# Gate products of a two-layer encoder: results kept in PSUM banks, the sigmoid table loaded earlier, products issued in a fixed order

## The chip, the core and the metric

The kernel runs on one core of one Trainium2 chip. A core has five engines with their own queues, each working strictly in its own order: TensorE (PE, matmuls; its weight loads are listed apart as PEld), VectorE (DVE), ScalarE (ACT), GpSimd (POOL) and SyncE (SP), which here only issues DMA transfers. Matmuls write into PSUM banks; everything else lies in SBUF. The metric is the device time of one execution in microseconds (us).

## The reference, and what is computed

The model is a trunk of two layers over 512 tokens of width 1024. Each layer adds the output of a token mixer (neighbourhood attention in layer 0, latent attention in layer 1) to the residual, and then adds a gated embedding. A final RMSNorm follows. The part that this case is about:

```python
h = x + y
gate = jax.nn.sigmoid(rmsnorm(h, ple_norm[i]) @ ple_w_gate[i])
x = h + gate * (p[i] @ ple_w_proj[i])
...
return rmsnorm(x, final_norm)
```

All is float32. The kernel splits every operand of a matmul into a rounded part ("hi") and the remainder ("lo") and computes hi x hi + lo x hi + hi x lo.

## The kernel before, in words

Layer 0 and the attention of layer 1 fill the first 600 us or so and are not touched. In layer 1 the gate's matmul `rmsnorm(h) @ ple_w_gate` (512 x 1024 by 1024 x 1024) is done with seven products of quarter size in place of eight (`gate_seven`, L571). The 512 rows are two halves of two row tiles; `i` = 0, 1 is the row tile within a half. Each product `p` has a left operand `X[p]` (a quarter of the turned `h`, or a sum or difference of quarters) and a right operand `W[p]` (a quarter of the weight, or a sum of quarters that was added up in DRAM earlier). They run in the order 1, 7, 6, 5, 4, 3, 2.

What feeds them:

- `out_proj` (L416) is the projection before it: its matmuls go out at L107, its sums into `res` at L428, and after each piece `turn_h` (L1011) multiplies by the gain (L1016), transposes on TensorE (L139, tag "T" of PSUM) and hands the bank to `keep_half` (L541), which copies or adds the quarters (L553 to L562). `operand` (L532) makes the hi part on ACT (L538) and the lo part on DVE (L539); `mixed` (L564) does so for products 6, 5, 4 and 3, with one more subtraction (L568) for 3.
- `prep` (L578) fetches the two pieces of a weight: a DMA from SP's queue into one of three buffers `wraw`, the hi part on ACT (L589), the lo part on POOL (L590). A buffer is free again when POOL has read it. The loop at L612 calls `prep` three products ahead.
- The matmuls (L634): twelve for each product and row tile, 512 columns wide. For products 1 and 2 of row tile 1 the columns are cut into two halves of 256.

What becomes of them: product 1 is copied out by ACT (`s1`, L639); product 7 is added to it by DVE (`s17`, L644); product 6 is copied out by ACT (`s6`, L647), and product 5 then goes on accumulating in the bank of 6 (tag "S"), and product 3 in the same bank again; product 2 goes on in the bank of product 1 (tag "mm", and "O" for the last half). `quarter` (L602) adds or subtracts the needed sums (L604, DVE), and `finish` (L593) does the rest of one quarter: the sigmoid (L594, ACT, scaled by the row's inverse norm `rh`), the load of the projection's piece `pe` (L596, SP), the product (L597, DVE) and the sum into the residual `r` (L599, DVE). The result of L604, L594 and L597 is a tile `g` in SBUF. Last, `done` (L1049) sums the squares of the finished row (L1060 on ACT, L1056 on DVE for the very last half), collects the mean (L1061), multiplies by the final gain (L1064 on POOL for the half of a row that is ready first, L1071 on DVE for the other), takes the power -0.5 on POOL (L1070), scales on ACT (L1072) and sends the row out (L1073, L1074).

The order of work on each engine isn't the order of the program's text. The Tile layer orders the instructions with a planning run of its own; `issue_after(x)` forbids it to place an instruction ahead of `x`. PSUM tiles are taken from rings by tag: "mm" has two banks, "S" two, "T" three, "O" one; a tile waits until the last reader of the tile that had its bank is through.

In the kernel before, the planning run mixes products on TensorE: ten of the twelve matmuls of product 6, row tile 0, go before product 7, parts of product 4 between those of product 6, and product 4 of row tile 0 before product 5.

Of the kernel before, what the change touches and what calls it, by code (L numbers as in the profile page):

```python
# [13 lines left out]
F32 = mybir.dt.float32  # L14
F32R = mybir.dt.float32r
AF = mybir.ActivationFunctionType
ALU = mybir.AluOpType
AX = mybir.AxisListType
PSUM = bass.MemoryType.PSUM
P = 128  # L20
S = 512
# [19 lines left out]
class Trunk:  # L41
# [374 lines left out]
    def out_proj(self, wap, oT, res, after, last_mm):  # L416
        nc = self.nc
        for n in range(2):
            ws = [self.load_w(wap[n, c], 1024, extra=n == 1 or c == 3) for c in range(4)]
            for u, t in enumerate((0, 2, 1, 3) if n and self.wxn > 5 else range(NT)):  # L420
                ps = self.psum(("mm", "mm", "S", "S", "T", "O", "mm", "mm")[n * NT + u])
                L = lambda s, k: oT[s][k // 4][:, k % 4, t * P:(t + 1) * P]
                W = lambda s, k: ws[k // 2][s][:, (k % 2) * S:(k % 2 + 1) * S]
                m = self.by_chunk(L, W)
                with self.tc.issue_after(last_mm):
                    self.mms(ps, m)
                r = res[t][:, n * S:(n + 1) * S]
                nc.vector.tensor_tensor(out=r, in0=ps, in1=r, op=ALU.add)  # L428
                after(t, n)
# [141 lines left out]
    def gate_seven(self, pool, layer, rh, res, after):  # L571

        nc = self.nc
        pieces = 0
        turns = 3 + self.wxn // 2
        W, A, Bk, s1, s17, s6 = {}, {}, {}, {}, {}, {}

        def prep(p):  # L578
            nonlocal pieces
            W[p] = []  # L580
            src = self.quarter[layer][p] if p < 4 else self.sums[layer][p]
            for c in range(2):
                own = pieces % turns < 3
                pieces += 1
                raw = self.wp.tile([P, 1024], F32, name="wraw", tag="wraw", bufs=3)
                q, n = (self.wp, 3) if own else (pool, self.wxn)
                hi, lo = (q.tile([P, 1024], F32R, name=t, tag=t if own else "w4", bufs=n) for t in ("whi", "wlo"))
                nc.sync.dma_start(raw, src[c * P:(c + 1) * P])
                nc.scalar.activation(hi, raw, AF.Copy)  # L589
                nc.gpsimd.tensor_tensor(out=lo, in0=raw, in1=hi.bitcast(F32), op=ALU.subtract)  # L590
                W[p].append((hi, lo))

        def finish(t, n, x, src, o=0, wd=S):  # L593
            nc.scalar.activation(x, src, AF.Sigmoid, scale=rh[t])  # L594
            pe = pool.tile([P, S], F32, name="pe", tag="pe", bufs=4)[:, :wd]
            nc.sync.dma_start(pe, self.pe[layer][t][:, n * S + o:n * S + o + wd])  # L596
            nc.vector.tensor_tensor(out=x, in0=pe, in1=x, op=ALU.mult)  # L597
            r = res[t][:, n * S + o:n * S + o + wd]
            nc.vector.tensor_tensor(out=r, in0=r, in1=x, op=ALU.add)  # L599
            after(t, n, o, wd)  # L600

        def quarter(t, n, ps, other, op):  # L602
            x = pool.tile([P, S], F32, name="g", tag="hg", bufs=3)
            nc.vector.tensor_tensor(out=x, in0=ps, in1=other, op=op)  # L604
            finish(t, n, x, x)

        order = (1, 7, 6, 5, 4, 3, 2)
        whole, parts = ((0, S),), ((0, 256), (256, 256))
        for p in order[:3]:
            prep(p)  # L610
        self.mixed(6)
        for k, p in enumerate(order):  # L612
            if k + 3 < len(order):
                prep(order[k + 3])
            if 0 < k < 4:
                self.mixed(order[k + 2])
            x = self.X[p]
            for i in range(2):
                cuts = parts if layer == 1 and i == 1 and p < 3 else whole
                if p == 1:  # L620
                    A[i] = [self.psum("O" if o else "mm") for o, wd in cuts]
                elif p in (7, 6, 4):
                    ps = self.psum({7: "T", 6: "S", 4: "T"}[p])
                    if p == 6:
                        Bk[i] = ps
                else:
                    ps = Bk[i]
                for h, (o, wd) in enumerate(cuts):
                    if p < 3:
                        ps = A[i][h]  # L630
                    m = [(x[:, 2 * s + i, k * P:(k + 1) * P], W[p][k // 2][r][:, k % 2 * S + o:k % 2 * S + o + wd])
                         for c in range(2) for s, r in ((0, 0), (1, 0), (0, 1)) for k in (2 * c, 2 * c + 1)]
                    for j, (l, r) in enumerate(m):
                        nc.tensor.matmul(ps[:, :wd], l, r, start=j == 0 and p in (1, 7, 6, 4),  # L634
                                         stop=j == 11 and p not in (1, 6, 5), skip_group_check=True)
                    if p == 1:
                        if o == 0:
                            s1[i] = self.temp("s1")
                        nc.scalar.activation(s1[i][:, o:o + wd], ps[:, :wd], AF.Copy)  # L639
                    elif p == 2:  # L640
                        finish(i, 0, pool.tile([P, S], F32, name="g", tag="hg", bufs=3)[:, :wd], ps[:, :wd], o, wd)
                    elif p == 7:
                        s17[i] = self.temp("s17")
                        nc.vector.tensor_tensor(out=s17[i], in0=ps, in1=s1[i], op=ALU.add)  # L644
                    elif p == 6:
                        s6[i] = self.temp("s6")
                        nc.scalar.activation(s6[i], ps, AF.Copy)  # L647
                    elif p == 5:
                        quarter(2 + i, 1, ps, s17[i], ALU.subtract)
                        nc.gpsimd.tensor_tensor(out=s6[i], in0=s17[i], in1=s6[i], op=ALU.subtract)  # L650
                    elif p == 4:
                        quarter(2 + i, 0, ps, s6[i], ALU.add)
                    else:
                        quarter(i, 1, ps, s1[i], ALU.subtract)

    def mla_c(self, pool, xT, cT, sets):
        nc, a = self.nc, self.a
# [533 lines left out]
```

## Time and profile before

| what | time |
|---|---|
| median of 3 runs | 670.32 us (670.09 to 671.56) |
| the profiled execution | 669.8 us |
| its span on the core | 668.0 us |
| PE / DVE / ACT / POOL busy | 652.5 / 383.1 / 422.3 / 421.4 us |
| mean granted clock of TensorE | 0.991 |

The profile is of one execution. Its page lists busy time by engine, the span in slices, the chain of waits that ended last, and groups of instructions. The timeline has one row for each run of equal instructions: start and length in us, engine, line of the code, operation, result and inputs, shapes, count, and in brackets how long the engine was idle before it and what ended that. A row of the view of stretches has the stretch, its length, and busy time and count of PE, PEld, DVE, ACT and POOL, then the granted TensorE clock, the DMA share and GB/s.

### The profile page before, as it was taken

To read this page: it belongs to the slowest core of one execution; us is meant where nothing else is said; L and a number is where in the kernel's file an instruction comes from. 1 tells how busy PE (TensorE), PEld (TensorE's weight loads), DVE (VectorE), ACT (ScalarE), POOL (GpSimd) and SP (SyncE) were. 2 spreads that over 40 slices of the span, in tenths; PEclk is the share of its full clock that TensorE was granted. 3 is DMA by queue.
4 is the path that set the end of the run, shared out by engine and by line. 5 is a ranking of instruction groups with operands and counts; after the bars stand their busy time and mean duration, and the time that the engine had idled before them with its cause. 6 is when DMAs were issued, how large, how long until landed. Compare 5 with 4: busy or idle time off the path is not lost.

```text
span 668.0 us, 10021 instructions
## 1 busy us (share of the span) xinstructions
PE 652.5 (98%) x3443; PEld 555.5 (83%) x3443; DVE 383.1 (57%) x817; ACT 422.3 (63%) x837; POOL 421.4 (63%) x340
## 2 busy tenths in 40 slices
PE   9999999999999999999999999999999999999991
PEld 6888888988988888888899888888888888888881
DVE  6180375737645515544615514888888875067867
ACT  7661686848767742543434636888989887347745
POOL 0395466876575765943155616886969785858773
PEclk9999999999999999999999999999999999999996
DMA  9949323966142146533343244110301232764323
GB/s 330 335 150 350 135 92 99 201 155 156 58 142 76 64 148 245 190 104 137 107 115 108 90 120 141 54 46 25 90 7 69 60 111 95 275 235 163 131 79 142
DMA packets 37682, 90.63 MB, mean 136 GB/s; under 512 B 4416, under 2 KB 13376, under 8 KB 37568
## 3 DMA queue, kind: packets, MB, share of 16 engines
q1 hardware_dynamic: 33040, 85.02, 37.3%
q0 software_dynamic: 4160, 4.19, 4.0%
q10 hardware_dynamic: 432, 0.79, 0.3%
q8 instruction: 27, 0.44, 0.3%
q14 instruction: 23, 0.19, 0.1%
HBM read 78.45 MB, written 16.78 MB: 143 GB/s over the span
## 4 chain that ended last, share of the span: by engine, by line
PE 91%; DVE 2%; POOL 2%; issue 2%; DMA 1%; ACT 1%; POOLq 0%; DVEq 0%
PE ps_mm L107 42%; PE ps_S L107 13%; PE ps_mm L721 6%; PE ps_T L139 6%; PE ps_O L832 4%; PE ps_T L107 3%; PE ps_O L107 3%; PE ps_T L238 2%; PE ps_O L402 2%; PE ps_mm L184 2%; PE ps_T L390 2%; PE ps_S L354 1%; PE ps_S L353 1%; DVE r L599 1%; PE ps_O L238 1%
## 5 line engine op out<-in xcount | busy, mean ns | idle before, releaser
L84 POOL TENSOR_TENSOR wwlo<-wraw,wwhi 128x1024 fp32r<-128x1024 f32 (+5 forms) x93 | 178.6, 1934 | 106.3 <-ACT wwhi L83 91.4
L83 ACT ACTIVATE wwhi<-wraw 128x1024 fp32r<-128x1024 f32 (+5 forms) x94 | 79.1, 863 | 74.4 <-PE ps_mm L107 18.3
L817 POOL TENSOR_TENSOR ex<-ex,rc 128x512 f32<-128x512 f32 x64 | 65.9, 1038 | 24.8 <-DVE rc L816 18.1
L815 ACT ACTIVATE ex<-ps_S,mx 128x512 f32<-128x512 f32 x64 | 44.0, 688 | 11.9 <-DVE mx L813 10.8
L813 DVE TENSOR_REDUCE mx<-ps_S 128x1 f32<-128x512 f32 x64 | 43.7, 682 | 6.8 <-PE ps_S L107 6.2
L96 DVE TENSOR_TENSOR pt_lo<-ps_T,pt_hi 128x512 fp32r<-128x512 f32 x64 | 43.2, 681 | 7.6 <-ACT pt_hi L94 7.3
L376 POOL TENSOR_TENSOR ex<-ex,rc 128x128 f32<-128x128 f32 (+1 forms) x64 | 34.8, 582 | 18.2 <-DVE rc L372 18.2
L107 PE MATMUL ps_mm<-xh,wwhi 128*128 128x512 f32 x152 | 40.9, 399 | 0.0
L94 ACT ACTIVATE pt_hi<-ps_T 128x512 fp32r<-128x512 f32 x64 | 37.7, 595 | 4.1 <-PE ps_T L139 3.8
L590 POOL TENSOR_TENSOR wlo<-wraw,whi 128x1024 fp32r<-128x1024 f32 x14 | 36.4, 2619 | 3.2 <-ACT whi L589 3.2
L139 PE MATMUL ps_T<-ident,ex 128*128 128x128 f32 x256 | 38.4, 272 | 0.0
L107 PE MATMUL ps_mm<-xl,wwhi 128*128 128x512 f32 x152 | 38.3, 391 | 0.0
L107 PE MATMUL ps_mm<-xh,wwlo 128*128 128x512 f32 x152 | 38.0, 390 | 0.0
L139 PEld LDWEIGHTS ps_T<-ident,ex 128*128 128x128 f32 x256 | 31.5, 140 | 7.7 <-POOL ex L817 0.4
L107 PE MATMUL ps_mm<-wwhi,hnT 128*128 128x512 f32 x128 | 35.0, 392 | 0.0
L205 DVE TENSOR_TENSOR u<-ps_O,u 64x512 f32<-64x512 f32 x32 | 22.0, 686 | 20.1 <-ACT u L204 19.6
L107 PEld LDWEIGHTS ps_mm<-xl,wwhi 128*128 128x128 f32 x152 | 28.4, 188 | 5.9
L107 PEld LDWEIGHTS ps_mm<-xh,wwlo 128*128 128x128 f32 x152 | 28.3, 188 | 5.8
L370 ACT ACTIVATE ex<-ex,mx 128x128 f32<-128x128 f32 (+1 forms) x64 | 30.2, 474 | 1.8 <-DVE mx L360 0.8
L107 PEld LDWEIGHTS ps_mm<-xh,wwhi 128*128 128x128 f32 x152 | 27.4, 188 | 4.8
L107 PE MATMUL ps_S<-ke,qe 96*128 96x512 f32 x96 | 28.9, 407 | 0.0
L107 PE MATMUL ps_S<-ko,qo 128*128 128x512 f32 x96 | 28.9, 409 | 0.0
(423 smaller groups left out, 1783.4 us busy)
## 6 DMA issues: line engine op xcount, KB each, us to landing
wraw<-na_qk SPq DMA_DIRECT2D x16, 512.0 KB, 3.2
pe<-pe SPq DMA_DIRECT2D x31, 256.0 KB, 2.8
wraw<-gate SPq DMA_DIRECT2D x14, 512.0 KB, 3.2
wraw<-na_v SPq DMA_DIRECT2D x8, 512.0 KB, 3.3
wraw<-na_o SPq DMA_DIRECT2D x8, 512.0 KB, 3.3
wraw<-mla_z SPq DMA_DIRECT2D x8, 512.0 KB, 3.5
wraw<-mla_o SPq DMA_DIRECT2D x8, 512.0 KB, 3.4
wraw<-sum SPq DMA_DIRECT2D x8, 512.0 KB, 3.2
```

Source lines behind the costliest of these rows:

```text
L83: nc.scalar.activation(hi[:, c], raw[:, c], AF.Copy)
L84: f = lambda e, c=c: e.tensor_tensor(out=lo[:, c], in0=raw[:, c], in1=hi[:, c].bitcast(F32), op=ALU.subtract)
L94: self.last_copy = nc.scalar.activation(hi, src, AF.Copy, scale=scale)
L96: nc.vector.tensor_tensor(out=lo, in0=src, in1=hi.bitcast(F32), op=ALU.subtract)
L107: last = self.last_mm = nc.tensor.matmul(out, l, r, start=i == 0, stop=i == n - 1)
L139: self.last_mm = self.nc.tensor.transpose(t[:, i * P:(i + 1) * P], b, self.ident)
L376: self.last_norm = nc.gpsimd.tensor_tensor(out=e, in0=e, in1=rc[:, qt:qt + 1].to_broadcast([P, e.shape[1]]), op=ALU.mult)
L590: nc.gpsimd.tensor_tensor(out=lo, in0=raw, in1=hi.bitcast(F32), op=ALU.subtract)
L721: self.last_mm = nc.tensor.matmul(PS[key], *terms[i], start=i == 0, stop=i == len(terms) - 1)
L813: nc.vector.reduce_max(mx, sp, axis=AX.X, negate=True)
L815: nc.scalar.activation(ex, sp, AF.Exp, bias=mx, accum_out=sm)
L817: nc.gpsimd.tensor_tensor(out=ex, in0=ex, in1=rc.to_broadcast([P, S]), op=ALU.mult)
```

## The change

It has these parts:

- `finish` works in place: sigmoid, product with `pe` and the sum's input stay in the PSUM bank that `quarter` (or product 2's matmuls) left them in. For products 4 and 3 the sum of the quarter is written back into the product's own bank; for product 5 it is written into a new bank of tag "T", since product 3 goes on accumulating in product 5's bank. The SBUF tile `g` is gone.
- A one-column sigmoid `warm` stands in front of the loop, so the sigmoid table is loaded there and not at the first quarter's sigmoid.
- Each matmul of the products carries `issue_after` of the one before it, and the first that of `out_proj`'s last: TensorE issues the products in the loop's order.
- The `prep` of a product is called one turn of the loop later for the last three (product 4's, 3's and 2's): before, `order[k + 3]` at turn k; now product 5 at turn 0, and `order[k + 2]` from turn 2 on.

```diff
-                    self.mms(ps, m)
+                    self.last_out = self.mms(ps, m)
...
-        def finish(t, n, x, src, o=0, wd=S):
-            nc.scalar.activation(x, src, AF.Sigmoid, scale=rh[t])
+        def finish(t, n, x, o=0, wd=S):
+            nc.scalar.activation(x, x, AF.Sigmoid, scale=rh[t])
...
-        def quarter(t, n, ps, other, op):
-            x = pool.tile([P, S], F32, name="g", tag="hg", bufs=3)
+        def quarter(t, n, x, ps, other, op):
             nc.vector.tensor_tensor(out=x, in0=ps, in1=other, op=op)
-            finish(t, n, x, x)
-
+            finish(t, n, x)
+
+        mm = self.last_out
...
         self.mixed(6)
+        warm = self.small.tile([P, 1], F32, name="warm", tag="warm", bufs=1)
+        nc.scalar.activation(warm, rh[3], AF.Sigmoid)
         for k, p in enumerate(order):
-            if k + 3 < len(order):
-                prep(order[k + 3])
+            if k == 0:
+                prep(order[3])
+            if k > 1 and k + 2 < len(order):
+                prep(order[k + 2])
...
-                        nc.tensor.matmul(ps[:, :wd], l, r, start=j == 0 and p in (1, 7, 6, 4),
-                                         stop=j == 11 and p not in (1, 6, 5), skip_group_check=True)
+                        with self.tc.issue_after(mm.ins):
+                            mm = nc.tensor.matmul(ps[:, :wd], l, r, start=j == 0 and p in (1, 7, 6, 4),
+                                                  stop=j == 11 and p not in (1, 6, 5), skip_group_check=True)
...
-                        finish(i, 0, pool.tile([P, S], F32, name="g", tag="hg", bufs=3)[:, :wd], ps[:, :wd], o, wd)
+                        finish(i, 0, ps[:, :wd], o, wd)
...
-                        quarter(2 + i, 1, ps, s17[i], ALU.subtract)
+                        quarter(2 + i, 1, self.psum("T"), ps, s17[i], ALU.subtract)
...
-                        quarter(2 + i, 0, ps, s6[i], ALU.add)
+                        quarter(2 + i, 0, ps, ps, s6[i], ALU.add)
...
-                        quarter(i, 1, ps, s1[i], ALU.subtract)
+                        quarter(i, 1, ps, ps, s1[i], ALU.subtract)
```

In the built programs the engines' orders are the same up to the products. From there: TensorE has the last four transposes (L139) right behind product 1 and the products in the loop's order. On ACT the table load and `warm` stand behind the hi part of product 4's second weight piece, which itself now comes behind the hi part of `X[6]`, row tile 1. On DVE the two subtractions from the last transposes (L560, L561) and the second L568 stand ahead of the lo parts of `X[4]` and `X[3]`, row tile 0; further on, L597 and L599 of one quarter follow each other directly, where before several quarters' steps were interleaved. POOL's order is the same. On SP the load of the last `pe` piece (256 columns) stands behind two output transfers.

More of the change, by code (lines that the diff above doesn't have):

```diff
@@ L589, in prep @@
                 nc.scalar.activation(hi, raw, AF.Copy)
-                nc.gpsimd.tensor_tensor(out=lo, in0=raw, in1=hi.bitcast(F32), op=ALU.subtract)
+                nc.gpsimd.tensor_tensor(out=lo, in0=raw, in1=hi.bitcast(F32),
+                                                                             op=ALU.subtract)
                 W[p].append((hi, lo))
-        def finish(t, n, x, src, o=0, wd=S):
-            nc.scalar.activation(x, src, AF.Sigmoid, scale=rh[t])
+        def finish(t, n, x, o=0, wd=S):
+            nc.scalar.activation(x, x, AF.Sigmoid, scale=rh[t])
             pe = pool.tile([P, S], F32, name="pe", tag="pe", bufs=4)[:, :wd]
```

## The prediction, made before the changed kernel was run

> **What bounds the kernel now.** I read the page first, then the stretches of the last 50 us, because the order of instructions before about 613 us is the same in both kernels on every engine; only the quarter products and what follows them change.
>
> ```profile
> 630.00:640.00 10.00, 10.00 (x46) 8.28 (x45) 3.04 (x5) 6.57 (x9) 8.57 (x5) 1.00 0.24 86
> 650.00:660.00 10.00, 3.61 (x28) 3.29 (x26) 9.77 (x19) 7.16 (x16) 5.48 (x5) 0.83 0.40 145
> ```
>
> After the stretch and its length come PE, weight load, VectorE (DVE), ScalarE (ACT) and GpSimd (POOL). TensorE is full at 630 to 640, at a granted clock of 1.00, and has 3.61 us of work left after 650 (its last row, below, ends at 653.6); the span ends at 668.0. So some 14 us are a tail, in which DVE is full (9.77 of 10), while at 630 to 640 it was busy only 3.04. DVE starts late, and then works slowly. The timeline says why:
>
> ```profile
> 636.99 0.69 DVE L604 TENSOR_TENSOR g<-ps_S,s 128x512 f32<-128x512 f32 x1 [4.64 <-PE ps_S L634]
> 637.62 1.06 ACT L589 ACTIVATE whi<-wraw 128x1024 fp32r<-128x1024 f32 x1 [3.40 <-POOL s L650]
> 638.70 1.28 ACT L594 ACT_TABLE_LOAD   x1
> 640.00 0.72 ACT L594 ACTIVATE g<-g,rs 128x512 f32<-128x512 f32 x1
> 640.75 1.02 DVE L597 TENSOR_TENSOR g<-pe,g 128x512 f32<-128x512 f32 x1 [3.08 <-ACT g L594]
> 641.81 2.77 DVE L599 TENSOR_TENSOR r<-r,g 128x512 f32<-128x512 f32 x1
> 641.18 2.85 POOL L590 TENSOR_TENSOR wlo<-wraw,whi 128x1024 fp32r<-128x1024 f32 x1
> 646.03 1.22 DVE L597 TENSOR_TENSOR g<-pe,g 128x512 f32<-128x512 f32 x1 [0.19 <-ACT g L594]
> 650.85 1.12 DVE L599 TENSOR_TENSOR r<-r,g 128x512 f32<-128x512 f32 x1
> 656.38 1.63 DVE L599 TENSOR_TENSOR r<-r,g 128x512 f32<-128x512 f32 x1
> 659.54 1.42 DVE L599 TENSOR_TENSOR r<-r,g 128x256 f32<-128x256 f32 x1
> 661.35 0.41 DVE L599 TENSOR_TENSOR r<-r,g 128x256 f32<-128x256 f32 x1
> 661.92 0.49 DVE L1056 CUSTOM_DVE_ANT_0 sq<-r,mn 128x256 f32<-128x256 f32 x1
> 662.49 0.99 POOL L1070 TENSOR_TENSOR rs<-mn,half 128x1 f32<-128x1 f32 x1 [0.33 <-DVE mn L1056]
> 663.52 0.75 DVE L1071 SCALAR_TENSOR_TENSOR r<-r,rs,gn 128x512 f32<-128x512 f32 x1 [0.44 <-POOL rs L1070]
> ```
>
> The first quarter's sum is there at 637.68, yet its sigmoid starts at 640.00, behind a weight piece and a table load on ACT. Then L599 takes 2.77 us for what L604 does in 0.69. It ends at 644.58, and the POOL row that it overlaps at 644.03: 0.55 later. Wherever a DVE operation with both inputs in SBUF meets a POOL operation, it ends some 0.55 after POOL; L604, with one input in PSUM, never stretches.
>
> **The change, part by part.** Below, P5.0 means product 5 for row tile i = 0.
>
> *Results in PSUM.* Sum, sigmoid and product of each quarter now stand in a bank, so L597 and L599 each have one SBUF input. What the six stretched rows lose goes: 0.34 + 2.09 + 0.54 + 0.44 + 0.95 + 1.01 = 5.4 us (each against 0.68, the last against 0.41). All six lie in the stretches where DVE is full. Not all of it reaches the end, because the matmuls and the handovers come next; the walk below finds how much.
>
> *Price of an operand in PSUM.* The groups by form give, behind the bar, busy us and the mean ns of one:
>
> ```profile
> L594 ACT ACTIVATE g<-ps_mm,rs 128x512 f32<-128x512 f32 x1 | 0.7, 667 | 0.0
> L594 ACT ACTIVATE g<-ps_mm,rs 128x256 f32<-128x256 f32 x1 | 0.5, 462 | 0.0
> ```
>
> No row of this trace has DVE or ACT writing PSUM. The nearest below: the same sigmoid reads PSUM in 0.67 and SBUF in 0.72, so 0.05 less. Above: the dearest untouched DVE form, L1071, takes 0.75 against 0.68, so 0.07 more. I take zero, since L604 from PSUM (0.69) stands nearest to what L597 and L599 become. Some 24 such operations lie on the path, so the ends are -1.2 and +1.7 us.
>
> [...]
>
> *Order on TensorE.* The products now run strictly 1, 7, 6, 5, 4, 3, 2; before, matmuls of 4 and 6 were mixed in. In order, one late operand holds everything behind it. I walk it with the rows:
>
> ```profile
> 619.33 1.09 PE L634 MATMUL ps_S<-whi,X 128*128 128x512 f32 x4
> 621.40 0.60 PE L139 MATMUL ps_T<-ident,hg 128*128 128x128 f32 x4
> 636.79 1.07 PE L634 MATMUL ps_S<-whi,X 128*128 128x512 f32 x4
> 639.51 0.84 PE L634 MATMUL ps_T<-whi,X 128*128 128x512 f32 x3
> 650.58 0.64 PE L634 MATMUL ps_mm<-whi,X 128*128 128x256 f32 x4
> 652.01 0.64 PE L634 MATMUL ps_O<-whi,X 128*128 128x256 f32 x4
> 653.21 0.40 PE L634 MATMUL ps_O<-wlo,X 128*128 128x256 f32 x2
> 616.60 2.31 DVE L1016 SCALAR_TENSOR_TENSOR hg<-r,rowb,gp 128x512 f32<-128x512 f32 x1
> 621.83 0.68 DVE L568 TENSOR_TENSOR b<-b,mix 128x512 f32<-128x512 f32 x1
> 625.84 0.67 DVE L560 TENSOR_TENSOR mix<-mix,ps_T 128x512 f32<-128x512 f32 x1
> 622.89 2.48 POOL L590 TENSOR_TENSOR wlo<-wraw,whi 128x1024 fp32r<-128x1024 f32 x1
> 622.89 5.31 POOL L590 TENSOR_TENSOR wlo<-wraw,whi 128x1024 fp32r<-128x1024 f32 x2
> ```
>
> A block of twelve is 639.51 - 636.79 = 2.72; a half block 652.01 - 650.58 = 1.43. P1 ends at 619.33 as before. The last transposes move up from 621.40 to there (their hg is ready at 618.91), +0.45; P7 to 625.2; P6.0 to 628.0. On DVE L560 now stands right behind L568: 622.4 instead of 625.84. L561 to 623.6; the second L568 is held by POOL until 625.37 + 0.55 = 625.9, the X lo part for P4.0 by POOL's next piece until 628.20 + 0.55 = 628.75; those for P3.0 and P6.1 follow by 629.95. P6.1 has its hi matmuls to 628.4 and waits: a new stall of 1.5. It ends at 632.2 (the copy s6, which P5.0 needs out of its bank, ends on ACT about 631.9), P5.0 at 634.9, P5.1 at 637.6, P4.0 at 640.4.
>
> *Table load early.* Its 1.28 leaves the gap before 640.00 and stands behind the second weight piece of product 4, ahead of what feeds POOL:
>
> ```profile
> 627.21 0.60 ACT L562 ACTIVATE d<-ps_T 128x512 f32<-128x512 f32 x1
> 628.71 0.66 ACT L538 ACTIVATE X<-mix 128x512 fp32r<-128x512 f32 x1
> 630.27 2.03 ACT L589 ACTIVATE whi<-wraw 128x1024 fp32r<-128x1024 f32 x2
> 631.43 2.59 POOL L590 TENSOR_TENSOR wlo<-wraw,whi 128x1024 fp32r<-128x1024 f32 x1 [3.23 <-ACT whi L589]
> 636.33 1.29 POOL L650 TENSOR_TENSOR s<-s,s 128x512 f32<-128x512 f32 x1
> 637.59 2.39 POOL L590 TENSOR_TENSOR wlo<-wraw,whi 128x1024 fp32r<-128x1024 f32 x1
> ```
>
> ACT after: X hi for P6.1 at 623.1 (L560 is earlier), weight piece to 624.7, load to 626.0, warm 0.25 (no row has one column; between nothing and the 0.46 of 256 columns), L562 to L538 1.5 as in the rows, L538 to L589 1.56: product 3's first piece at 629.3, where it was 630.27. So the load's new cost is covered by L560's earlier start; without that cover it would cost its 1.28. POOL's piece runs 630.4 to 632.8. Its end frees the buffer of the last weight piece, whose L589 came 637.62 - 634.02 = 3.6 later: 636.4, ending 637.45 (before 638.68).
>
> But POOL now works while DVE still makes X lo parts. After 629.95: s17 0.6; X for P5.1 held to 632.8 + 0.55 = 633.35; s17 to 633.95; X for P3.1 held by the next piece (to 635.7) to 636.25; X for P4.1 held by L650 (1.29) to 638.05. Only then L604 of P5.0, though its matmuls ended at 634.9. Sigmoid 638.7 to 639.4, L597, and L599 ends at 640.75, not 644.58.
>
> *The bank wait.* The tag T has three banks. P5.0's sum takes one, and P4.1's matmuls get the same one, so they wait for that L599: 640.8 instead of 640.4, a stall of 0.4. TensorE then ends its blocks at 643.5, 646.2, 649.0, 651.7, 653.1 and 654.55: 1.1 later than before (653.45).
>
> *The tail.* Two ACT rows, and the page's row of the loads of pe:
>
> ```profile
> 644.61 0.63 ACT L1060 ACTIVATE sq<-r 128x512 f32<-128x512 f32 x1 [3.89 <-DVE r L599]
> 645.27 1.34 ACT L594 ACTIVATE g<-g,rs 128x512 f32<-128x512 f32 x2
> pe<-pe SPq DMA_DIRECT2D x31, 256.0 KB, 2.8
> ```
>
> One quarter's Square (0.66 to the next sigmoid), sigmoid 0.72, L597 0.60, L599 0.68 with handovers is 2.7, about a block. L599 ends at 643.45 and 646.2; the fourth, with L1071 and one L604 put before it, at 650.2. From there DVE is full: L597, L599 and L604 of products 3 and 2 (seven at 0.60 with the overlap of neighbours, four halves at 0.33, one L1071 at 0.67, five small at 0.11, waits 0.4) and L1056 (0.57 with its read) bring 657.9. The end follows as now: POOL's power and L1071 ended 664.27 - 662.41 = 1.86 after L1056. That is 659.8, where 664.27 was: 4.4 less. The output transfers behind (3.7 to 668.0) stay.
>
> On SP's queue the last pe piece moves behind two output transfers: it is issued about 651 and lands 2.8 later, 653.8; L597 wants it at 656.2. Nothing. POOL's order is unchanged.
>
> Sum: span 668.0 - 4.4 = 663.6, profiled execution 669.8 - 4.4 = 665.4; the median of the runs stands 0.5 above that execution, so 670.32 - 4.4 = **665.9 us**.
>
> **Rivals.** *More gain* (0.13): DVE passes between POOL's pieces, and neither stall of TensorE (1.5 and 0.4) comes. The blocks end at 652.65, and from the last matmul a sigmoid, L597, L599, L1056 and 1.86 cannot take less than 3.9: 656.5, or 662.5 us at the least; I put it at 663.8. For it: the L568 at 621.83 passed in 0.68, just ahead of POOL's next piece. Against: POOL was busy 8.57 of 10 at 630 to 640.
>
> *Dearer operands* (0.14): PSUM operands at the upper end, +1.7: 667.6, to 668.5 if the table load also loses its cover. For it: no row shows such writes. Against: L604.
>
> *Slower* (0.08): the bank wait. P4.1 starts when P5.0's L599 ends, and everything on TensorE is behind it. From L604 to that L599 took 644.58 - 636.99 = 7.6 before; here I count 2.75. Were it still 7.6, it would end at 645.6, TensorE 4.8 later, the kernel at 670.7. It decides from 645.2 on, each microsecond one more: were the last weight piece on ACT, which stands ahead of the sigmoid, also late, 672. Against: two thirds of the 7.6 are the load and the stretched rows.
>
> *No change* (0.04): the end is set by something that the change leaves alone, 670.3. Against: DVE's full tail.
>
> **How the numbers follow.** Forecast 0.61, with a range of its own of 664.3 to 667.5; rivals as given. The range for all, 663.5 to 669.0, leaves out the slower case, no change and the edges of the others. A measurement of this kernel tells about 0.2% (1.3 us) from no change. Faster: 0.61 + 0.13 + 0.12 of the dearer case = 0.86; the same: 0.04 + 0.02 = 0.06; slower 0.08.
>
> **What would show it.** L597 and L599 at 0.7 all through; no table load behind 630; L604 of P5.0 near 638 and its L599 near 641; TensorE idle about 1.5 in P6.1 and little before P4.1, last matmul near 654.7; last L1071 near 660. The prediction is wrong if L599 of P5.0 ends after 643, if DVE or ACT rows with PSUM outputs take over 0.75, or if the stall in P6.1 passes 3 us.

## The result, and the profile after

The kernel before took 670.05 us (median of 8 runs, 669.83 to 671.56), the changed kernel 668.52 us (median of 8, 668.13 to 669.39): a ratio of 0.9976, 95% interval 0.9965 to 0.9987. It is 1.5 us faster. 4.4 us were forecast. The profiled execution took 669.19 us, with a span of 667.4, where the one before had 669.8 and 668.0.

The line numbers have moved: the quarter products' matmuls are L640 (L634 before), the sigmoid L595 (L594), the product with `pe` L598 (L597), the sum into r L600 (L599), the last scaling L1077 (L1071); L604 is still the quarter's sum.

The stretches of the changed kernel, with the columns as before (stretch, length, PE, weight load, DVE, ACT, POOL, clock, DMA share, GB/s):

```profile
630.00:640.00 10.00, 8.62 (x37) 6.67 (x36) 10.00 (x9) 5.94 (x11) 7.72 (x4) 1.00 0.37 127
640.00:650.00 10.00, 9.23 (x40) 7.25 (x40) 5.93 (x12) 4.20 (x9) 9.16 (x6) 1.00 0.16 54
650.00:660.00 10.00, 8.58 (x49) 7.26 (x47) 9.21 (x20) 7.49 (x17) 3.36 (x4) 1.00 0.43 157
```

DVE is busy 5.93 of 10 at 640 to 650 although POOL is at 9.16: no row of L598 or L600 is stretched any more (the longest of 128x512 took 0.70). But TensorE still has 8.58 us of work behind 650, where it had 3.61. It ends late; and it also began late. First the timeline of before, its first quarter product, then that of the changed kernel:

```profile
613.62 1.17 PE L634 MATMUL ps_mm<-whi,X 128*128 128x512 f32 x4
```

```profile
616.19 1.17 PE L640 MATMUL ps_mm<-whi,X 128*128 128x512 f32 x4
632.72 0.72 PE L640 MATMUL ps_S<-whi,X 128*128 128x512 f32 x2 [1.39 <-DVE X L539]
639.42 0.69 DVE L604 TENSOR_TENSOR ps_T<-ps_S,s 128x512 f32<-128x512 f32 x1
641.23 1.06 ACT L589 ACTIVATE whi<-wraw 128x1024 fp32r<-128x1024 f32 x1 [5.28 <-DMA wraw<-gate]
642.19 0.64 ACT L595 ACTIVATE ps_T<-ps_T,rs 128x512 f32<-128x512 f32 x1
643.60 0.69 DVE L600 TENSOR_TENSOR r<-r,ps_T 128x512 f32<-128x512 f32 x1
644.43 1.17 PE L640 MATMUL ps_T<-whi,X 128*128 128x512 f32 x4 [0.77 <-DVE r L600]
658.19 0.39 PE L640 MATMUL ps_O<-wlo,X 128*128 128x256 f32 x2
662.90 0.75 DVE L1077 SCALAR_TENSOR_TENSOR r<-r,rs,gn 128x512 f32<-128x512 f32 x1 [0.44 <-POOL rs L1076]
```

The first quarter product starts 2.57 us later than before, although no instruction that stands ahead of it was changed or moved. I call "stage" the time from that matmul to the end of the last L1071 or L1077. Before it is 664.27 - 613.62 = 50.65 us; now 663.65 - 616.19 = 47.46. So the changed stage gained 3.19 us, and the part of the kernel that the change leaves alone lost 2.57. The prediction's stage was 659.8 - 613.62 = 46.2.

### The profile page after: what moved, and what is told of

It is laid out like the page before. It is cut to its first block, busy times and chain, and to the rows that moved or that the text cites. A ratio compares the mean times of both kernels' runs of the same rounds, so it can differ in the third digit from the quotient of the medians.

```text
span 667.4 us, 10026 instructions
## 1 busy us (share of the span) xinstructions
PE 655.5 (98%) x3443; PEld 555.3 (83%) x3443; DVE 382.8 (57%) x817; ACT 422.0 (63%) x838; POOL 420.8 (63%) x340
## 4 chain that ended last, share of the span: by engine, by line
PE 91%; DVE 3%; ACT 2%; DMA 2%; issue 1%; POOL 1%; POOLq 0%; ACTq 0%
PE ps_mm L107 42%; PE ps_S L107 13%; PE ps_mm L727 7%; PE ps_T L139 6%; PE ps_O L838 4%; PE ps_T L107 3%; PE ps_O L107 3%; PE ps_T L238 2%; PE ps_O L402 2%; PE ps_mm L184 2%; PE ps_T L390 2%; PE ps_S L354 1%; PE ps_S L353 1%; PE ps_O L238 1%; DMA wraw<-gate 1%
## 5 line engine op out<-in xcount | busy, mean ns | idle before, releaser
L823 POOL TENSOR_TENSOR ex<-ex,rc 128x512 f32<-128x512 f32 x64 | 66.3, 1046 | 25.2 <-DVE rc L822 18.1
L107 PE MATMUL ps_mm<-xh,wwhi 128*128 128x512 f32 x152 | 40.8, 399 | 0.0
L139 PE MATMUL ps_T<-ident,ex 128*128 128x128 f32 x256 | 38.4, 272 | 0.0
L107 PE MATMUL ps_mm<-xl,wwhi 128*128 128x512 f32 x152 | 38.2, 390 | 0.0
L107 PE MATMUL ps_mm<-xh,wwlo 128*128 128x512 f32 x152 | 38.1, 391 | 0.0
L139 PEld LDWEIGHTS ps_T<-ident,ex 128*128 128x128 f32 x256 | 31.5, 140 | 7.7 <-POOL ex L823 0.4
L107 PE MATMUL ps_mm<-wwhi,hnT 128*128 128x512 f32 x128 | 35.5, 396 | 0.0
L107 PEld LDWEIGHTS ps_mm<-xl,wwhi 128*128 128x128 f32 x152 | 28.4, 188 | 5.8
L107 PEld LDWEIGHTS ps_mm<-xh,wwlo 128*128 128x128 f32 x152 | 28.3, 188 | 5.8
L107 PEld LDWEIGHTS ps_mm<-xh,wwhi 128*128 128x128 f32 x152 | 27.4, 188 | 4.7
L107 PE MATMUL ps_S<-ke,qe 96*128 96x512 f32 x96 | 29.2, 410 | 0.1
L107 PE MATMUL ps_S<-ko,qo 128*128 128x512 f32 x96 | 28.9, 409 | 0.0
```

The lines of the kernel that those rows point to most:

```text
L107: last = self.last_mm = nc.tensor.matmul(out, l, r, start=i == 0, stop=i == n - 1)
L139: self.last_mm = self.nc.tensor.transpose(t[:, i * P:(i + 1) * P], b, self.ident)
L823: nc.gpsimd.tensor_tensor(out=ex, in0=ex, in1=rc.to_broadcast([P, S]), op=ALU.mult)
```

## The experiments

Two questions: what made the 613 us ahead of the change slower, and which part of the change carries the gain behind them. In this table, "first" is the start of the first quarter product, "pitch" the mean time from start to start over 16 matmuls of `out_proj` near 600 us (rows below). Ratios are to the kernel before on the same chip.

| kernel | first, us | stage, us | pitch, ns | ratio (95%) |
|---|---|---|---|---|
| before | 613.62 | 50.65 | 228.1 | 1 |
| after | 616.19 | 47.46 | 233.3 | 0.9976 (0.9965 to 0.9987) |
| after_again | 616.84 | 46.85 | | 0.9971 (0.9959 to 0.9983) |
| e1_no_shift | 613.61 | 46.61 | 228.1 | 0.9943 (0.9927 to 0.9960) |
| e1_again | 614.22 | 46.23 | | 0.9939 (0.9925 to 0.9953) |
| e2_before_shifted | 616.50 | 50.92 | 233.4 | 1.0033 (1.0021 to 1.0044) |
| e3_shift_64 | 615.87 | 46.90 | 228.8 | 0.9944 (0.9928 to 0.9960) |
| e4_shift_128 | 617.13 | 47.21 | 233.4 | 0.9977 (0.9968 to 0.9986) |
| m1_no_psum | 614.31 | 52.12 | | 1.0032 (1.0019 to 1.0045) |
| m2_no_order | 615.78 | 50.37 | | 0.9999 (0.9990 to 1.0008) |
| m3_no_warm | 613.85 | 48.82 | | 0.9981 (0.9972 to 0.9989) |
| p1_psum_only | 614.10 | 51.64 | | 1.0013 (1.0004 to 1.0021) |
| b1_early_raw | 613.49 | 45.19 | | 0.9920 (0.9906 to 0.9933) |

### Where the first 613 us lost 2.6 us

Theory L puts the late start on the layout of SBUF, theory D on the drift of a single execution. First the changed kernel once more, as it was, on the chip of the next three:

> The changed kernel once more, as the yardstick for the runs beside it. Theory L (layout): the new one-column tile moves every SBUF tile that is allocated behind it by 32 bytes, and matmuls whose moving operand lies there run at about 0.233 us in place of 0.227, ahead of the changed stage too; then the first matmul of the quarter products starts near 616 us again, where it was 613.6 before. Theory D (drift): that delay of 2.6 us belonged to one execution; then it starts near 613.6 this time. Time by both: 668.5 as measured, give or take 0.7.

The late start came again, 616.84 us, which speaks against D. The median was 668.83 us.

The new tile `warm` has one column, but it takes a slot of its own of 32 bytes in each partition, in the pool of small tiles. In the built programs every tile allocated behind that pool stands 32 bytes further: the weight halves under the tag "w4" at 162240 instead of 162208, the residual r at 137664 instead of 137632. Tiles of the large pools (weights from 111520 on) stay. e1_no_shift is the changed kernel with `warm` in a ring that was there already, so that all addresses are those of before, and every engine's order is that of the changed kernel:

```diff
-        warm = self.small.tile([P, 1], F32, name="warm", tag="warm", bufs=1)
+        warm = self.small.tile([P, 1], F32, name="warm", tag="mn")
```

> The changed kernel, with the tile of the early sigmoid taken from a ring of small tiles that exists already, so that no address moves; every engine's order is that of the changed kernel. Theory L: the quarter products start near 613.6, their blocks of twelve matmuls take 2.72 us and not 2.80, and the time falls by 2.6 for the stages before and about 0.5 for the blocks, to 665.4. Theory D: 668.5, as the changed kernel.

e2_before_shifted is the kernel before with an unused tile in that pool (and one small memset), ahead of the products:

```diff
+        pad = self.small.tile([P, 1], F32, name="pad", tag="pad", bufs=1)
+        nc.vector.memset(pad, 0.0)
         for k, p in enumerate(order):
```

> The kernel before, with nothing but an unused one-column tile in the place of the early sigmoid's tile (one memset of one column on VectorE comes with it), so that the later tiles move by the same 32 bytes. Theory L: slower by about 3 us, 673, with the quarter products starting near 616. Theory D: 670.1, as before.

Then the changed kernel with a wider slot, 64 bytes and later 128:

```diff
-        warm = self.small.tile([P, 1], F32, name="warm", tag="warm", bufs=1)
+        warm = self.small.tile([P, 16], F32, name="warm", tag="warm", bufs=1)[:, :1]   # e3_shift_64
+        warm = self.small.tile([P, 32], F32, name="warm", tag="warm", bufs=1)[:, :1]   # e4_shift_128
```

> The changed kernel with that tile 16 columns wide, so that the later tiles move by 64 bytes in place of 32. Theory L has two forms. L1, the place within 64 bytes counts: as without a shift, 665.4. L2, any move away from the places of the kernel before costs: 668.5 or more. Theory D: 668.5.

> The changed kernel with a tile of 32 columns in the place of the one-column tile: everything behind it stands 128 bytes further than in the kernel before, not 32. If the distance from a 128-byte boundary decides: start-to-start 226.6 to 227 ns in all groups, as in e1_no_shift, the first quarter product within 0.3 us of 613.6 (a stall of the early weight pieces taken off), ratio 0.993 to 0.996. If any move costs: 228 to 233 ns in the moved groups, 1 to 2.6 us later at the first quarter product, ratio 0.995 to 0.998.

> The kernel of e1_no_shift once more, to size the shift by more executions. Theory L (the 32-byte shift costs the changed kernel 2.4 to 2.6 us ahead of the first quarter product and 0.3 to 0.8 behind it): the first quarter product at 613.4 to 613.9 us where no stall of the early weight pieces (77 us) comes, the lowest time near 665.6, the median 665.6 to 667.4, ratio 0.993 to 0.996. If the one low time of the first series was chance: a median of 668 or more, ratio above 0.9965, and the shift would be worth less than 1 us in the time.

The same stretch of `out_proj`'s matmuls in the timelines. Between the starts of the two rows lie the same 16 matmuls, with no idle time. The first column is the start, the second the length. First the kernel before, then the changed one, e1_no_shift, e3_shift_64 and e4_shift_128:

```profile
600.80 1.08 PE L107 MATMUL ps_T<-ww,o1h 128*128 128x512 f32 x4
...
604.45 0.62 PE L107 MATMUL ps_T<-ww,o1l 128*128 128x512 f32 x2
```

```profile
603.06 1.10 PE L107 MATMUL ps_T<-ww,o1h 128*128 128x512 f32 x4
...
606.80 0.63 PE L107 MATMUL ps_T<-ww,o1l 128*128 128x512 f32 x2
```

```profile
600.78 1.08 PE L107 MATMUL ps_T<-ww,o1h 128*128 128x512 f32 x4
...
604.43 0.62 PE L107 MATMUL ps_T<-ww,o1l 128*128 128x512 f32 x2
```

```profile
602.96 1.07 PE L107 MATMUL ps_T<-ww,o1h 128*128 128x512 f32 x4
...
606.62 0.62 PE L107 MATMUL ps_T<-ww,o1l 128*128 128x512 f32 x2
```

```profile
604.00 1.10 PE L107 MATMUL ps_T<-ww,o1h 128*128 128x512 f32 x4
...
607.74 0.63 PE L107 MATMUL ps_T<-ww,o1l 128*128 128x512 f32 x2
```

3.65 us before, 3.74 after, 3.65 with the old addresses, 3.66 with 64 bytes, 3.74 with 128: the same instructions, in the same order, at one granted clock (1.00), with another start address of the operand that streams through (the first of the two inputs, `ww`); the operand that is loaded (`o1h`, `o1l`) stayed. One matmul costs 5.2 ns more, 2.3%. Over all neighbouring matmuls of L107 with 512 columns ahead of the products (start to start, where that is under 260 ns), the two traces give: 392 with the streaming operand moved and the one being loaded for the next matmul not, 227.9 ns before and 233.3 after; 872 with neither moved, 227.7 and 227.7. The first kind alone is 2.1 of the 2.6 us. A block of twelve in the changed stage took 2.80 us instead of 2.72.

The place of the streaming operand alone is not the whole of it. Near the start of the kernel 31 matmuls have both operands in moved tiles. Before, then after:

```profile
9.38 0.85 PE L107 MATMUL ps_T<-whi 128*128 128x512 f32 x3
...
16.41 0.39 PE L107 MATMUL ps_O<-whi,wlo 128*128 128x512 f32 x1
```

```profile
9.33 0.84 PE L107 MATMUL ps_T<-whi 128*128 128x512 f32 x3
...
16.36 0.40 PE L107 MATMUL ps_O<-whi,wlo 128*128 128x512 f32 x1
```

7.03 us both times, 226.8 ns each. So it may be the distance between the two operands that counts. No run moves them apart on purpose, and in the attention of layer 1 matmuls with both moved (`ke` with `qe`) rose from 231.7 to 234.0 ns.

So the shift is the cause: alone it makes the kernel before 0.33% slower (e2), and taking it out of the changed kernel gains as much (0.9976 and 0.9971 against 0.9943 and 0.9939, about 2.2 us of median). The median of e1_no_shift, 667.32 us (665.55 to 668.49), lies above the 665.4 that theory L said. Its profile is of an execution of 665.75 us, so its stage speaks for the fast end of that spread. e1_again excludes that the low time was chance: its median is 666.44 us (665.95 to 666.52) where before stood at 670.68. Theory L holds, D falls. What remains open is the law. That every move costs the same fails on the 64 bytes, which cost almost nothing in these rows; the median there, 667.62 us, fits neither of the two forms of L. That the distance from a boundary of 64 or 128 bytes decides fails on the 128 bytes, which cost as much as 32.

Some of the spread of single executions has another place. In m2_no_order's timeline one early matmul waits 1.64 us for L270 on DVE; the copy on ACT that L270 needs (L267) starts at 76.5, where it started at 74.3 before. I put this down to a weight piece that lands late:

```profile
78.73 2.06 PE L107 MATMUL ps_mm<-xh,wwhi 128*128 128x512 f32 x8 [1.64 <-DVE sb L270]
```

Everything after it is 1.9 us later. The profiled executions have between 0 and 1.9 us of this: before, after and e1_no_shift none, after_again 0.5, e4_shift_128 0.8, e3_shift_64 1.1 (so its shift costs about 1.1 of its 2.25). That is why the column "first" must be read with the pitch beside it, and why the stage is the better measure of the parts.

### What the parts are worth

Theory P says that results in PSUM carry the gain, theory O that the order and the early load do. Three kernels each leave out one part and keep the old addresses; the fourth has the first part alone. m2_no_order leaves out two parts at once, the fixed order and the later calls of `prep`. Their edits, in the same order, against the changed kernel and (p1) against the kernel before:

```diff
 m1_no_psum: results in SBUF again
-        def quarter(t, n, x, ps, other, op):
+        def quarter(t, n, ps, other, op):
+            x = pool.tile([P, S], F32, name="g", tag="hg", bufs=3)
...
 m2_no_order: the planner orders the products, prep as before
-                        with self.tc.issue_after(mm.ins):
-                            mm = nc.tensor.matmul(ps[:, :wd], l, r, start=j == 0 and p in (1, 7, 6, 4),
+                        nc.tensor.matmul(ps[:, :wd], l, r, start=j == 0 and p in (1, 7, 6, 4),
...
 m3_no_warm: the table is loaded at the first quarter's sigmoid
-        warm = self.small.tile([P, 1], F32, name="warm", tag="warm", bufs=1)
-        nc.scalar.activation(warm, rh[3], AF.Sigmoid)
...
 p1_psum_only: the kernel before with the results in PSUM
-                        quarter(2 + i, 1, ps, s17[i], ALU.subtract)
+                        quarter(2 + i, 1, self.psum("T"), ps, s17[i], ALU.subtract)
```

> The changed kernel without its first part, and with the addresses of before: sums, sigmoids and products with pe go back to SBUF tiles, the fixed order and the early table load stay. Theory P (the gain of the changed stage comes from results in PSUM, because VectorE no longer meets GpSimd with both inputs in SBUF): L597 and L599 stretch again whenever a GpSimd piece runs, 3 to 5 us of stretch in sum over the stage, and the last r ends 2.5 to 4 us later behind the first quarter product than in e1_no_shift (46.6): a stage of 49 to 50.5 us, a ratio to the kernel before of 0.998 to 1.002. Theory O (order and load carry it): the stage stays within 1 us of 46.6 and the ratio near 0.994.

> The changed kernel without its fixed order, and with the addresses of before: results in PSUM and the early table load stay, the matmuls of the quarter products stand in the planner's order. Theory P: the fixed order is worth nothing of its own; the stage stays within 1 us of e1_no_shift's 46.6, the stalls of TensorE (0.7 in P6.1, 0.4 to 1.2 before P4.1) become smaller or move, ratio 0.992 to 0.996. Theory O: without the order the quarters come late, the stage is 1.5 to 4 us longer, ratio 0.997 to 1.000.

> The changed kernel without the early table load (and so without its tile, with the addresses of before): results in PSUM and the fixed order stay, the load of 1.28 us stands again before the first sigmoid. Theory P: the load costs 1.28 us on ScalarE ahead of the first sigmoid, but the weight pieces ahead of it come up to 1.3 us earlier, so L599 of P5.0 ends 0 to 1.3 us later than in e1_no_shift (27.3 behind the first matmul), and the stage is 46.3 to 47.9 us, ratio 0.993 to 0.9965. Theory O: the early load is worth its 1.28 us or more: a stage of 47.9 or more, ratio above 0.9965.

> The kernel before with results in PSUM alone: no fixed order, table load at the first sigmoid, the addresses of before. If the stretched rows are the whole cost, as the prediction's 5.4 us read it: L597 and L599 at 0.7 all through, stage 46.5 to 48 us where it was 50.65, ratio 0.993 to 0.996. If the parts pay only together (as without the order the stage was 50.4): the rows are unstretched and the stage stays at 49.5 to 51, ratio 0.998 to 1.001, because the quarters of products 4 and 3 then reach the tail together with those of product 2.

Against e1's stage of 46.6 us, leaving out PSUM costs 5.5 (52.1), the order with the calls of `prep` 3.8 (50.4), the early load 2.2 (48.8). These sum to far more than the 4.0 that all three gain, and PSUM without the order is not a gain at all: 51.6, ratio 1.0013. Theory P was right on m1 (which came out even longer than it said) and wrong on m2 and m3; theory O was wrong on m1 and right on the other two; of p1's two readings the second came, a little beyond its range. Results in PSUM and the order pay only together. Each trace says why.

*PSUM.* m1_no_psum has the stretched rows again. Two of its lines, and then the changed kernel's; the columns behind the count are the least, median and longest ns of one:

```profile
L597 DVE TENSOR_TENSOR g<-pe,g x9: 419/693/1426, 640.4 to 663.0; 128x512 f32<-128x512 f32 x7, 128x256 f32<-128x256 f32 x2
...
L599 DVE TENSOR_TENSOR r<-r,g x9: 418/692/1805, 641.4 to 663.5; 128x512 f32<-128x512 f32 x7, 128x256 f32<-128x256 f32 x2
```

```profile
L598 DVE TENSOR_TENSOR ps_T<-pe,ps_T x4: 695/696/697, 642.9 to 651.3; 128x512 f32<-128x512 f32 x4
...
L600 DVE TENSOR_TENSOR r<-r,ps_T x4: 678/686/687, 643.6 to 653.1; 128x512 f32<-128x512 f32 x4
L600 DVE TENSOR_TENSOR r<-r,ps_S x2: 678/678/679, 655.3 to 657.5; 128x512 f32<-128x512 f32 x2
```

Summed over these two lines, DVE spends 17.0 us in m1_no_psum, 16.5 before, and 11.3 in e1_no_shift and p1_psum_only. With the order, the 5.7 us between m1 and e1 reach the end almost whole (5.5 of stage). In the planner's order, the 5.2 between before and p1 reach it not at all. That order is not the one of before: with results in PSUM the planning run placed the products anew (below). Results in PSUM with before's own order were not run. At 640 to 650 of the changed kernel, where GpSimd is busy 9.16 of 10, no row of L598 or L600 passes 697 ns: each has one input in PSUM. In m1_no_psum, L599 with both inputs in SBUF starts at 658.19, when a GpSimd row of 1.26 us has begun at 658.12; it takes 1.74 us and ends 0.55 behind it.

*The order.* Without it (m2 and p1 have the same order on TensorE) 18 of the 36 matmuls of product 2 go ahead of product 4, mixed among those of products 5 and 3. So the last whole quarter, that of product 3's second row tile, comes later and together with product 2's pieces. The end of m2_no_order on DVE:

```profile
655.68 0.69 DVE L603 TENSOR_TENSOR ps_S<-ps_S,s 128x512 f32<-128x512 f32 x1
...
657.47 1.01 DVE L599 TENSOR_TENSOR r<-r,ps_mm 128x512 f32<-128x512 f32 x2
...
659.33 1.42 DVE L1072 SCALAR_TENSOR_TENSOR r<-r,rs,gn 128x512 f32<-128x512 f32 x1
660.74 0.67 DVE L599 TENSOR_TENSOR r<-r,ps_S 128x512 f32<-128x512 f32 x1
661.33 0.41 DVE L599 TENSOR_TENSOR r<-r,ps_O 128x256 f32<-128x256 f32 x1
```

and the same work in e1_no_shift:

```profile
651.12 0.69 DVE L604 TENSOR_TENSOR ps_S<-ps_S,s 128x512 f32<-128x512 f32 x1
...
654.03 0.68 DVE L600 TENSOR_TENSOR r<-r,ps_S 128x512 f32<-128x512 f32 x1
...
655.56 1.01 DVE L600 TENSOR_TENSOR r<-r,ps_mm 128x512 f32<-128x512 f32 x2
...
657.22 0.41 DVE L600 TENSOR_TENSOR r<-r,ps_O 128x256 f32<-128x256 f32 x1
```

The last quarter's sum stands 655.68 - 615.78 = 39.9 us behind the first matmul without the order, 651.12 - 613.61 = 37.5 with it, and its sum into r 45.6 against 41.1. In m2, one L1072 also takes 1.42 us where the others take 0.75.

*The early load.* Its own 1.28 us are not what m3_no_warm loses. That kernel at the same place; the last row is the view of stretches:

```profile
629.04 5.43 POOL L590 TENSOR_TENSOR wlo<-wraw,whi 128x1024 fp32r<-128x1024 f32 x2 [0.72 <-ACT whi L589]
629.39 2.83 DVE L539 TENSOR_TENSOR X<-mix,X 128x512 fp32r<-128x512 f32 x1
632.27 0.73 PE L638 MATMUL ps_S<-whi,X 128*128 128x512 f32 x2 [3.48 <-DVE X L539]
633.64 1.91 PE L638 MATMUL ps_S<-whi,X 128*128 128x512 f32 x4
630.00:640.00 10.00, 7.72 (x27) 6.20 (x28) 10.00 (x7) 4.45 (x6) 10.00 (x5) 0.83 0.26 90
```

Without the load, ACT delivers the next weight piece earlier, GpSimd starts on it at 629.04, and the lo part of X that P6.1 needs is caught (2.83 us). TensorE waits 3.48 us, where it waits 1.32 in e1_no_shift. There GpSimd starts on that piece at 630.36, when this lo part is through (the matmul that waited for it starts at 629.87): the load on ACT held it back. The clock was lower too: at 630 to 640, which holds most of the wait, 0.83 was granted, where e1_again has 1.00, and the four matmuls at 633.64 took 1.91 us where others take 1.07. So the last matmul ends 44.5 us behind the first, 3.1 later than in e1, and 2.2 of that reach the end. All this is luck of the order, not a saved load: between p1 and m2, where TensorE's waits are alike (0.8 and 0.9 us in both), the early load is worth 51.64 - 50.37 = 1.27, its own length.

### The last weight piece

The chain of the changed kernel holds a transfer, in the middle of what the prediction had walked (start us, length, what):

```profile
633.19 2.95 POOL wlo L590
636.16 5.04 DMA wraw<-gate
641.23 1.06 ACT whi L589
642.29 0.56 ACT ps_T L595
```

The last weight piece can be fetched only when a GpSimd piece has freed its buffer, and the first sigmoid stands behind its hi part on ACT. b1_early_raw is e1_no_shift with one thing more: this piece's raw data goes, in two halves, into buffers that the transposes have left free.

```diff
+                early = p == 2 and c == 1
...
+                    rw = pool.tile([P, S], F32, name="hraw", tag="hg", bufs=3) if early else raw
+                    nc.sync.dma_start(rw, src[c * P:(c + 1) * P, s])
```

> e1_no_shift with one thing more: the raw data of the last weight piece go into two halves that the transposes have left free, so that its transfer need not wait for the end of a GpSimd piece (5.1 us from that end to the weight piece on ScalarE in the changed kernel, against the 3.6 that the prediction took). If that transfer sets the first sigmoid, as the chain of waits says: the piece stands on ScalarE before 637, the first sigmoid follows L604 (2 to 3 us earlier behind the first matmul), L599 of P5.0 ends at 25.5 to 26.5 instead of 27.3, TensorE's stall before P4.1 goes, and the stage is 45 to 46 us, ratio 0.990 to 0.993. If it does not (DVE's order around the X lo parts sets L604 anyway, or the tail is full): the stage stays at 46.6 and the ratio at 0.994.

The profile of b1_early_raw (the sigmoid is L598 here, the sum into r L603):

```profile
632.39 1.17 ACT L593 ACTIVATE whi<-hraw 128x512 fp32r<-128x512 f32 x2
636.49 0.69 DVE L607 TENSOR_TENSOR ps_T<-ps_S,s 128x512 f32<-128x512 f32 x1
637.21 0.66 ACT L598 ACTIVATE ps_T<-ps_T,rs 128x512 f32<-128x512 f32 x1 [3.17 <-DVE ps_T L607]
638.63 0.69 DVE L603 TENSOR_TENSOR r<-r,ps_T 128x512 f32<-128x512 f32 x1
```

The sigmoid follows the quarter's sum at once; the sum into r ends 25.8 us behind the first matmul (27.3 in e1), the stall before P4.1 is gone, the stage is 45.2 us. 664.42 us, median of 5 (664.32 to 664.78), ratio 0.992: this version is faster than both kernels.

## Why the prediction was right or wrong

The step that failed is the first sentence: that "the order of instructions before about 613 us is the same in both kernels on every engine; only the quarter products and what follows them change". The order is the same. That the times are then the same was assumed, and the sum started from 613.62 without a term for it. The new tile moved what is allocated behind it, and that cost 2.6 us ahead of the stage and 0.08 us per block in it. The prediction's own sign, that it is wrong if L599 of P5.0 ends after 643, came true for this reason: in the changed kernel that sum ends at 644.29, in e1_no_shift at 640.87. No rival had it: "No change" looked for an end that the change leaves alone, not for a start that it spoils. Without the shift the forecast is nearly met: 0.9941 (the mean of e1's two ratios) is 4.0 us less than before, where 4.4 were forecast, and the stage is 46.6 and 46.2, where 46.2 was forecast.

Point by point, behind the first matmul, for the forecast, e1_no_shift (old addresses) and the changed kernel, in us:

| step | forecast | e1 | after |
|---|---|---|---|
| TensorE's wait in P6.1 | 1.5 | 1.32 | 1.39 |
| L604 of P5.0 starts | 24.4 | 22.9 | 23.2 |
| last weight piece starts on ACT | 22.8 | 24.2 | 25.0 |
| first sigmoid starts | 25.1 | 25.2 | 26.0 |
| sum into r of P5.0 ends | 27.1 | 27.3 | 28.1 |
| wait before P4.1 | 0.4 | 0.42 | 0.77 |
| last matmul ends | 40.9 | 41.4 | 42.4 |
| stage | 46.2 | 46.6 | 47.5 |

- The 5.4 us of stretched rows vanish: right. The longest of these rows, 2.77 us, is now 0.69, and none passes 0.70.
- The price of PSUM operands, taken as zero: right. L598 takes 0.689 to 0.697 against 0.68 (+0.01 to +0.02), L600 0.678 to 0.687, and the sigmoid within PSUM 0.64 to 0.66 where it was 0.72 in SBUF. So the rival of dearer operands falls.
- The order: the two stalls it costs came as forecast. That it, with the later calls of `prep`, is worth 3.8 us beside results in PSUM was not seen: the walk used it in every step but never asked what the planner's order would make of the same rows.
- The early load: taken as covered, worth at most its 1.28. It is worth 2.2, because its place on ACT holds GpSimd away from P6.1's lo part, and so spares TensorE the wait of 3.48 us and the lower clock (0.83 at 630 to 640) that came with it in m3_no_warm.
- The last weight piece: mis-sized, 3.6 us from GpSimd's end to its hi part, 4.5 in e1 and 5.1 in the changed kernel. The first sigmoid was forecast to follow L604 and in fact followed this piece; since L604 came 1.5 us earlier than forecast, the two errors cancel in e1, which is luck, and in the changed kernel 0.9 us remain. b1 shows that the transfer was what held it.
- "Slower", the bank wait: its condition, L599 after 645.2, did not come (28.1 is 641.7 on the clock of before). Its argument has a wrong sum: the load and the stretched rows (1.28, 0.34 and 2.09) are 3.7 of the 7.6, half and not two thirds. The other rivals: TensorE's stalls came, so "More gain" falls.

## What to carry to other kernels

A tile of one column moved every tile allocated behind its pool by 32 bytes here, and the same 16 matmuls near 600 us then took 3.74 us in place of 3.65. Where TensorE is the bound, compare the addresses of the two built kernels, and the pitch of equal matmuls in the two traces, before any theory about the edit; put small additions into a ring that exists. Behind that: when a resource conflict is removed, ask which order lets the gain reach the end, since results in PSUM in the planner's order were worth nothing here, and with the fixed order 5.5 us.

## What the hardware showed

- The time of a matmul with 512 columns changed here with the place of its operands in SBUF. With the streaming operand moved and the loaded one not, it was 228.1 ns from start to start at the old address, 228.8 at 64 bytes further, 233.3 and 233.4 at 32 and 128; with both moved by 32 bytes it stayed at 226.8 in the 31 matmuls near the start. No run here explains the pattern.
- In m3_no_warm the granted clock was 0.83 at 630 to 640, a stretch that holds most of TensorE's wait of 3.48 us. In e1_no_shift the longest wait of this stage was 1.32 us, and the four matmuls at 630.90 behind it took 1.08 us; in e1_again, the same kernel, the clock at 630 to 640 was 1.00.
- A DVE operation with both inputs in SBUF that started while a GpSimd operation of 512 or 1024 columns ran ended behind it: 0.54 to 0.55 us with 512 columns (L597 and L599 in before, L599 at 658.19 in m1_no_psum), 0.28 to 0.29 with 256 (L599 at 659.54 in before, L597 at 661.24 in m1_no_psum).
- A transfer of 512 KB that landed 3.5 us from issue before took 5.0 in the changed kernel (4.5 in e1_no_shift, 4.1 in e1_again), though no other transfer of data was under way. The DMA view of 630 to 642 shows one packet of instructions in both, with its share of the engines doubled. Before, then after; behind the queue stand packets, MB and share of 16 engines, behind the issues the median from issue to landing, which for the two transfers of the changed kernel is the mean of 3.1 and 5.0:

```profile
q8 instruction: 1, 0.02, 0.5%
...
wraw<-gate SPq DMA_DIRECT2D x1, 512.0 KB, 3.5
```

```profile
q8 instruction: 1, 0.02, 1.0%
...
wraw<-gate SPq DMA_DIRECT2D x2, 512.0 KB, 4.1
```

That this packet is what delayed the transfer was not tested.
- ScalarE's sigmoid of 512 columns from a bank into the same bank took 0.64 to 0.66 us in the changed kernel, against 0.72 from SBUF into SBUF before.
